# Gates' one-hot products in the float32r form with 256 columns per token, a gather rate of 0.39 per load, x turned beside the first projection

## The chip, the cores and the metric

The kernel runs on one core of a Trainium2 chip. The metric is the device time in microseconds of one execution; several executions are taken and the median is quoted. A profile comes from one further execution. Five engines appear in it: PE (TensorE: matmuls, with its weight loads listed as PEld), DVE (VectorE), ACT (ScalarE), POOL (GpSimd) and SP (SyncE), the last of which only issues transfers here.

## The reference

One block of a transformer over 256 tokens of width 2048, all in 32-bit floats. Four steps follow one another, each adding to the residual `h` but the last:

```
n = rmsnorm(x, g);  proj = n @ w_in                      # 2048 x ~10,500
y_a = dilated windowed attention (3 dilations, 4 heads of 128)
y_b = gates * (compressed, selected and windowed attention; 16 heads of 64, 2 key groups)
h = x + (sigmoid(m0) * (y_a @ w_up_a) + sigmoid(m1) * (y_b @ w_up_b)) @ w_out
h = h + cross attention over 256 memory rows
# experts: 8 heads, 16 of 128 x 128 = 16384 experts per head and token
xn = rmsnorm(h);  eid, g = top16 of the product keys, softmax of the scores
h = h + sum_e g * gelu(xn . u_tab[eid]) * v_tab[eid]     # 128 experts per token
out = rmsnorm(h)
```

The two expert tables `u_tab` and `v_tab` have 16384 rows of 2048 floats each, 134 MB per table.

## The kernel before, in words

A planner orders the instructions: the program is traced in Python, each instruction gets its place by the order of tracing and by when the planner's model takes its inputs to be ready, and the engines then work through their queues strictly in the planned order. `issue_after` (used through `tc_after`) keeps an instruction behind a given one on the same engine.

**Start (`phase1`, L287 on).** x comes in four blocks of 512 columns, each in two token halves (L301). `gain_T` (L255) turns a block with eight transposes on PE; ACT writes the rounded high part times the gain, DVE the remainder, so that x stands as a pair of float32r operands (`nh`, `nl`), features on the partitions. All four blocks are turned first; then come the sums of squares (L215, L217), the reciprocal root (L228, POOL) and the row of it along the free axis (`rstd_row`, L232). The transposes need the constant `ident`, fetched on POOL's queue (L89).

**Projections.** `proj_col` (L184) and `proj_tok` (L155) run over units of 256 features: a 512 KB weight load into one of three `raw` buffers, a split on ACT (`wh`, L149) and DVE (`wl`, L150), and three products per tile (high x high, high x low, low x high). After each unit `tick` lets one background generator take a step: the turning of the memory input (`mem_T`, L350), then attention. In `item_b` (L577) one step computes the scores of four pairs (two key groups of 64 features on partitions 0 to 63 and 64 to 127, two branches), and a later one the values: products with 64 output rows, key group 0 on rows 0 to 63, key group 1 on 64 to 127, in the order group, branch, key tile (L581, L589, L630).

**Experts (`phase2`, L841).** The first 160 tokens (NA) go through both tables in full, as dense products: 256 loads of 512 KB per table, 8 matmuls of 160 columns to a load in 32-bit form (two records each). The products' results are multiplied with gates spread over all 128 x 128 experts (`spread`, L1065): for each token, a one-hot matrix of 128 x 128 for the first key and one for the second, weighted with the gate, are built on DVE (L1077, L1078), multiplied on PE (L1080, two records) into PSUM, four tokens to a bank, and taken out by ACT (L1085, L1087) or, where a table product is there already, by a multiplication on DVE (L1089, L1091). A tick takes one group of four tokens; there are 40 groups, spaced to end at load 236 of the first table.

The other 96 tokens are handled by indirect gathers: 96 gathers of 128 rows x 8 KB (1.05 MB) from each table, issued on POOL (L993), into four buffers. A gather of the first table is followed by a dot product on DVE (L998), one of the second by a weighted sum (L1008). A dot is traced three gathers after its fetch. With the row fetch and a fold near the end the list has 194 steps. `gtick` (L1046) runs after each load and takes `RATE` = 0.415 steps per load in the first table; at load 256 the rate is set so that the remaining steps are spread over 250 loads of the second table. The count `done` begins at 3. A gather waits for the matmul last issued at its place in the trace (`paced`, L973).

Table loads go on SP's queue into eight buffers (three `raw`, five others; `load`, L1166), each issued when PE has freed a buffer. Seven more loads of the first table are fetched during the last projections (L1107). The fold (L1018) adds the first gathered group's sums into the residual by matmuls while the second table is still running; the residual and the final gains are fetched back during the second table (L1235).

Of the kernel before, what the change touches and what calls it, by code (L numbers as in the profile page):

```python
# [9 lines left out]
F32 = mybir.dt.float32  # L10
# [19 lines left out]
NA = 160  # L30
# [5 lines left out]
RATE = 0.415  # L36
# [25 lines left out]
def setup(tc, I, out):  # L62
# [26 lines left out]
    nc.gpsimd.dma_start(c.ident[:], I["cst"][:, 0:128])  # L89
# [192 lines left out]
def phase1(c):  # L282
# [24 lines left out]
    for nb in range(4):  # L307
        last = gain_T(c, lambda hf, nb=nb: xsrc(hf, nb), N, 0, nb, c.pj, "pj")
    with tc_after(c, last):
        for nb in range(4):  # L310
            for hf in range(2):
                sumsq(c, ss, hf, nb, xsrc(hf, nb), tmp)
    rs0 = rstd_of(c, ss, "n0")
    row0 = rstd_row(c, rs0, trp, "tr", "row0")

    wq = I["w_in"]
    tk = lambda: tick(c)
    first_x(c, N)


    aq, ak, av = [], [], []
    for g in range(3):
        aq.append(page([128, 4, 256], f"aq{g}"))
    free.extend(s for _, s in xs)
# [4 lines left out]

    def to_cols(t, row):  # L330
        def f(i, ps):
            nc.vector.tensor_mul(t[:, 2 * i:2 * i + 2, :], ps[:], row[:, None, :].to_broadcast([128, 2, 256]))
        return f
# [16 lines left out]
    def mem_T():  # L350
        for _ in range(6):
            yield
        for nb in range(4):
            nc.sync.dma_start(mem[nb][0][:],
                              I["mem"][:, nb * 512:nb * 512 + 512].rearrange("(h p) f -> p h f", p=128))
            for _ in range(3):
                yield

        nc.sync.dma_start(dmask[:], cst[:, 384:1408].rearrange("p (a b) -> p a b", a=4))
        nc.sync.dma_start(cmask[:, 0:128], cst[:, 256:384])  # L360
        nc.sync.dma_start(cmask[:, 128:678], cst[:, 1408:1958])
        yield
        for nb in range(4):
            for q in range(2):
                gain_T(c, lambda hf, nb=nb: msrc(hf, nb), M, 2, nb, trp, "tr", (q,))
                yield
                yield
            for hf in range(2):
                sumsq(c, ssm, hf, nb, msrc(hf, nb), tmp)
            yield  # L370
        norm_m["rs"] = rstd_of(c, ssm, "nm")
        norm_m["row"] = rstd_row(c, norm_m["rs"], trp, "tr", "rowm")
        yield

    c.bg.append(mem_T())
    for g in range(3):
        proj_col(c, lambda u, b=g: wq[b, u], KT, N, to_cols(aq[g][0], row0), tk)
# [199 lines left out]
    def item_b(hf, r, sh):  # L577
# [3 lines left out]
        pairs = [(j, kt) for j in range(4) for kt in range(hf + 1)]  # L581
        v = {}

        def scores():
            sc = [scp.tile([128, 2, 256], F32, name="sc") for _ in range(2)]
            for g in range(2):
                p = slice(g * 64, g * 64 + 64)
                for br in range(2):
# [252 lines left out]
def phase2(c):  # L841
# [223 lines left out]
    def spread():  # L1065
# [3 lines left out]
        wtb = state["wtb"] = wbp.tile([128, 128 - NE1, NA], F32, name="wtb")  # L1069
        c.rate, c.n_tick = (NA // 4 + 1) / (236 - state["unit"]), 0  # L1070
        for n0 in range(0, NA, 4):
            gp = skp.tile([128, 4, 128], F32, name="gp")
            for j in range(4):
                n = n0 + j
                oh1 = sp.tile([128, 128], F32, name="oh1", bufs=6)
                oh2 = sp.tile([128, 128], F32, name="oh2", bufs=6)
                nc.vector.tensor_scalar(oh1[:], c.iota[:], eT[0][:, n:n + 1], None, ALU.is_equal)  # L1077
                nc.vector.tensor_scalar(oh2[:], c.iota[:], eT[1][:, n:n + 1], eT[2][:, n:n + 1],  # L1078
                                        ALU.is_equal, ALU.mult)
                nc.tensor.matmul(gp[:, j, :], oh1[:], oh2[:], start=True, stop=True)  # L1080
            gv = gp[:].rearrange("p n e -> p e n")
# [328 lines left out]
```

## Time and profile before

| | |
|---|---|
| time, median of 3 runs | 2163.99 us (2160.7 to 2164.49) |
| profiled execution, its own time | 2163.59 us |
| its span, first to last instruction | 2161.8 us, 36357 instructions |
| PE busy | 2119.6 us, 98% |
| PEld busy | 1999.1 us, 92% |
| DVE busy | 1250.0 us, 58% |
| ACT busy | 565.8 us, 26% |
| POOL busy | 261.7 us, 12% |
| moved by DMA | 642.15 MB, mean 297 GB/s |
| mean granted TensorE clock | 0.995 of 2.4 GHz |

The busy share counts the time in which an engine has an instruction in work. Matmuls overlap in PE's pipeline and their ends are modelled, so a PE that shows 100% can still be fed faster or slower; the spacing of its records tells its pace. The stages lie one behind the other: the first projection to about 43 us, the projections and both attentions to 545, the up, output, cross-attention and routing projections to 957, the first expert table to 1571.5, the second to 2131, and the end. The gates' products run from 1158.5 to 1513 us, inside the first table. A time for a group of instructions is busy time; idle time before it is put down to what was waited for.

### The profile page before, as it was taken

The page shows a single profiled execution, that of the slowest core. Times are in us where ns is not written, and L with a number is a line of the kernel's source. Part 1 is how long each engine was busy: PE and PEld are TensorE (multiplying, and loading weights), DVE is VectorE, ACT ScalarE, POOL GpSimd, SP SyncE. Part 2 cuts the span into 40 slices and gives each one's busy share as a digit, 9 for nine tenths or more (in the row PEclk, how much of TensorE's full clock was granted, in tenths as well). Part 3 has the DMA queues.
Part 4 walks back from the last instruction along what each step waited for, and adds up shares of the span by engine and source line. Part 5 has one row for each costly group of instructions (what it writes and reads, how often), then busy time and mean ns, then how long its engine had stood idle before and what let it go on. Part 6 is the DMA issues. An engine that isn't in the chain of part 4 may idle for free.

```text
span 2161.8 us, 36357 instructions
## 1 busy us (share of the span) xinstructions
PE 2119.6 (98%) x14602; PEld 1999.1 (92%) x14602; DVE 1250.0 (58%) x2326; ACT 565.8 (26%) x1277; POOL 261.7 (12%) x253
## 2 busy tenths in 40 slices
PE   8999999999999999999998999999999999999997
PEld 7998998778888888999998999999999999998996
DVE  5555655776575656766896666766443333333334
ACT  5445444556545555422111111000000000000001
POOL 0000000000000000013222121122221111111111
PEclk9999999999999999999999999999999999999999
DMA  7566545434655556588999999999999999998995
GB/s 246 176 195 190 163 137 171 146 127 137 195 175 188 186 168 219 198 267 346 401 408 405 401 397 395 401 403 391 413 414 412 412 414 413 411 410 337 411 403 200
DMA packets 151977, 642.15 MB, mean 297 GB/s; under 512 B 16928, under 2 KB 19136, under 8 KB 126848
## 3 DMA queue, kind: packets, MB, share of 16 engines
q1 hardware_dynamic: 120560, 425.99, 54.6%
q0 software_dynamic: 30528, 212.76, 24.6%
q8 instruction: 114, 1.87, 0.4%
q10 hardware_dynamic: 720, 1.08, 0.1%
q14 instruction: 55, 0.45, 0.1%
HBM read 635.57 MB, written 4.19 MB: 296 GB/s over the span
## 4 chain that ended last, share of the span: by engine, by line
PE 74%; issue 13%; DMA 6%; DVE 3%; POOL 3%; ACT 1%; POOLq 0%; ACTq 0%; DVEq 0%
PE up L1191 20%; PE y_b L1220 7%; PE pj L168 7%; PE pj L169 7%; PE pj L170 7%; PE pj L204 5%; PE pj L205 5%; PE pj L203 5%; PE y_s L1220 4%; DMA ga<-in_ur_dram,idx 3%; POOL ga L993 2%; PE gp L1080 1%; DVE ga L998 1%; DMA raw<-in_v_dram 1%; DMA ga<-in_vr_dram,idx 1%
## 5 line engine op out<-in xcount | busy, mean ns | idle before, releaser
L150 DVE TENSOR_TENSOR wl<-raw,wh 128x512 fp32r<-128x512 f32 (+1 forms) x576 | 391.2, 684 | 287.5 <-ACT wh L149 280.8
L1191 PE MATMUL up<-xr,raw 128*128 128x160 f32 x3968 | 549.3, 299 | 7.9 <-DMA raw<-in_u_dram 6.4
L1191 PEld LDWEIGHTS up<-xr,raw 128*128 128x128 f32 x3968 | 540.7, 190 | 10.0 <-DMA raw<-in_u_dram 6.2
L149 ACT CAST wh<-raw 128x512 fp32r<-128x512 f32 (+1 forms) x576 | 351.9, 616 | 400.7 <-PE pj L204 164.1
L1008 DVE SCALAR_TENSOR_TENSOR acc<-ga,a,acc 128x2048 f32<-128x2048 f32 x94 | 221.1, 2352 | 372.5 <-DMA ga<-in_vr_dram,idx 372.5
L998 DVE SCALAR_TENSOR_TENSOR ga<-ga,gx 128x2048 f32<-128x2048 f32 x96 | 219.9, 2290 | 148.8 <-DMA ga<-in_ur_dram,idx 148.5
L1220 PE MATMUL y_b<-wta,raw 128*128 128x160 f32 x1520 | 220.6, 300 | 1.7 <-DMA raw<-in_v_dram 1.7
L1220 PEld LDWEIGHTS y_b<-wta,raw 128*128 128x128 f32 x1520 | 210.8, 190 | 3.2 <-DMA raw<-in_v_dram 2.9
L205 PE MATMUL pj<-nh,wl 128*128 128x256 f32 x576 | 163.5, 285 | 0.2 <-DVE wl L150 0.2
L204 PE MATMUL pj<-nl,wh 128*128 128x256 f32 x576 | 163.6, 284 | 0.0
L993 POOL DMA_INDIRECT ga<-in_ur_dram,idx x96 | 120.2, 1252 | 352.5 <-PE up L1191 145.3
L993 POOL DMA_INDIRECT ga<-in_vr_dram,idx x96 | 100.3, 1045 | 503.0 <-PE y_b L1220 438.2
L203 PE MATMUL pj<-nh,wh 128*128 128x256 f32 x558 | 160.0, 287 | 0.0
L1220 PE MATMUL y_b<-wtb,raw 128*128 128x160 f32 x1040 | 151.8, 300 | 0.0
L168 PE MATMUL pj<-wh,nh 128*128 128x512 f32 (+1 forms) x384 | 150.0, 392 | 0.0
L1256 ACT COPY ysb<-y_s 128x480 f32<-128x480 f32 x1 | 0.6, 560 | 564.4 <-PE y_s L1220 564.4
L1220 PEld LDWEIGHTS y_b<-wtb,raw 128*128 128x128 f32 x1040 | 144.6, 190 | 3.7 <-issue 3.7
L169 PE MATMUL pj<-wl,nh 128*128 128x512 f32 (+1 forms) x384 | 147.5, 384 | 0.3 <-DVE wl L150 0.2
L170 PE MATMUL pj<-wh,nl 128*128 128x512 f32 (+1 forms) x384 | 147.0, 383 | 0.0
L1220 PE MATMUL y_s<-wta,raw 128*128 128x160 f32 x912 | 136.6, 299 | 1.4 <-DMA raw<-in_v_dram 1.4
L1220 PEld LDWEIGHTS y_s<-wta,raw 128*128 128x128 f32 x912 | 127.9, 190 | 2.1 <-DMA raw<-in_v_dram 2.1
L205 PEld LDWEIGHTS pj<-nh,wl 128*128 128x128 f32 x576 | 110.7, 193 | 1.4 <-DVE wl L150 0.7
(346 smaller groups left out, 2933.4 us busy)
## 6 DMA issues: line engine op xcount, KB each, us to landing
raw<-in_v_dram SPq DMA_DIRECT2D x256, 512.0 KB, 12.1
raw<-in_u_dram SPq DMA_DIRECT2D x249, 512.0 KB, 7.7
raw<-in_w_in_dram SPq DMA_DIRECT2D x160, 512.0 KB, 3.6
raw<-in_w_out_dram SPq DMA_DIRECT2D x32, 512.0 KB, 3.4
raw<-in_w_pq_dram SPq DMA_DIRECT2D x32, 512.0 KB, 4.3
raw<-in_w_up_b_dram SPq DMA_DIRECT2D x16, 512.0 KB, 3.4
raw<-in_w_xkv_dram SPq DMA_DIRECT2D x16, 512.0 KB, 3.4
raw<-in_w_up_a_dram SPq DMA_DIRECT2D x8, 512.0 KB, 3.4
```

The source lines that it names most:

```text
L149: c.last_act = nc.scalar.copy(h[:, :cols], raw[:, k, :cols]).ins
L150: c.last_sub = nc.vector.tensor_sub(l[:, :cols], raw[:, k, :cols], h[:, :cols].bitcast(F32)).ins
L168: nc.tensor.matmul(o, xh[:, s], h[:, :cols], start=kt == 0, stop=False)
L169: nc.tensor.matmul(o, xh[:, s], l[:, :cols], start=False, stop=False)
L170: c.last_mm = nc.tensor.matmul(o, xl[:, s], h[:, :cols], start=False, stop=kt == nk - 1).ins
L203: nc.tensor.matmul(o, h[:, s], xh, start=False, stop=False)
L204: nc.tensor.matmul(o, h[:, s], xl, start=False, stop=False)
L205: c.last_mm = nc.tensor.matmul(o, l[:, s], xh, start=False, stop=kt == nk - 1 and j % 2 == 1).ins
L993: paced(nc.gpsimd.indirect_dma_start(out=t[:], out_offset=None, in_=table, in_offset=bass.IndirectOffsetOnAxis(ap=g["idx"][:, i:i + 1], ax ...
L998: nc.vector.scalar_tensor_tensor(t[:], t[:], 1.0, g["x"][:], ALU.mult, ALU.mult, accum_out=g["a"][:, i:i + 1])
L1191: c.last_mm = c.last_sub = nc.tensor.matmul(ps[j][:, 0:NA], raw[:, k, j * 128:j * 128 + 128], x, start=kt == 0, stop=kt == KT - 1).ins
L1220: c.last_mm = c.last_sub = nc.tensor.matmul(o, raw[:, d // 4 % 2, d % 4 * 128:d % 4 * 128 + 128], wt, start=e == 0 and d % 3 == 0, stop=e ...
```

## The change

Six edits. `RATE` becomes 0.39. `ident` is fetched on SP's queue. The first of x's four blocks is turned before the first projection, the other three inside it (at its units 1, 3 and 5), with the sums of squares at unit 6 and the row at unit 7; the transposes' PSUM banks are four others than the projection's. That first projection takes no background steps, and `mem_T` no longer skips six. In `item_b` the two key groups alternate. In `spread` the gate is split once into a rounded high part and a remainder (`ghl`); for four tokens DVE builds the first one-hots in one operation, the second ones in one, and multiplies the second by both parts in two; PE multiplies in float32r form with 256 columns per token (high and low side by side), two tokens to a bank; ACT copies the low half out and DVE adds the high half, and the rest works from that sum in SBUF. The float32r operands and the sum lie in buffers that the weight splits used.

```diff
-RATE = 0.415
+RATE = 0.39
@@ setup
-    nc.gpsimd.dma_start(c.ident[:], I["cst"][:, 0:128])
+    nc.sync.dma_start(c.ident[:], I["cst"][:, 0:128])
@@ phase1
-    for nb in range(4):
-        last = gain_T(c, lambda hf, nb=nb: xsrc(hf, nb), N, 0, nb, c.pj, "pj")
-    with tc_after(c, last):
-        for nb in range(4):
-            for hf in range(2):
-                sumsq(c, ss, hf, nb, xsrc(hf, nb), tmp)
-    rs0 = rstd_of(c, ss, "n0")
-    row0 = rstd_row(c, rs0, trp, "tr", "row0")
+    stats = {}
+    turns = Banks(c.pp, ["tr", "pv", "s0", "s1"])
+
+    def x_T(nb):
+        stats["last"] = gain_T(c, lambda hf: xsrc(hf, nb), N, 0, nb, turns, "tx")
+
+    def ahead(u):
+        if u in (1, 3, 5):
+            x_T((u + 1) // 2)
+        if u == 6:
+            with tc_after(c, stats["last"]):
+                for nb in range(4):
+                    for hf in range(2):
+                        sumsq(c, ss, hf, nb, xsrc(hf, nb), tmp)
+            stats["rs"] = rstd_of(c, ss, "n0")
+        if u == 7:
+            stats["row"] = rstd_row(c, stats["rs"], trp, "tr", "row0")
...
+    x_T(0)
     first_x(c, N)
...
+    proj_col(c, lambda u: wq[0, u], KT, N, lambda i, ps: to_cols(aq[0][0], stats["row"])(i, ps), lambda: None, ahead)
+    rs0, row0 = stats["rs"], stats["row"]
...
     def mem_T():
-        for _ in range(6):
-            yield
...
-    for g in range(3):
+    for g in (1, 2):
         proj_col(c, lambda u, b=g: wq[b, u], KT, N, to_cols(aq[g][0], row0), tk)
@@ item_b
-        pairs = [(j, kt) for j in range(4) for kt in range(hf + 1)]
+        pairs = [(2 * g + br, kt) for br in range(2) for kt in range(hf + 1) for g in range(2)]
...
-            for g in range(2):
-                p = slice(g * 64, g * 64 + 64)
-                for br in range(2):
+            for br in range(2):
+                for g in range(2):
+                    p = slice(g * 64, g * 64 + 64)
                     nc.tensor.matmul(sc[g][:, br, :nk], bq[r // 4][0][p, r % 4, q0:q0 + 128],
                                      kvT[p, 2 + br, 0:nk], start=True, stop=True)
@@ spread
+        ghl = sp.tile([128, NA, 2], F32, name="ghl")
+        gh = sp.tile([128, NA], R, name="gh")
+        nc.scalar.copy(gh[:], eT[2][:])
+        nc.scalar.copy(ghl[:, :, 0], gh[:].bitcast(F32))
+        nc.vector.tensor_sub(ghl[:, :, 1], eT[2][:], gh[:].bitcast(F32))
...
-            gp = skp.tile([128, 4, 128], F32, name="gp")
-            for j in range(4):
-                n = n0 + j
-                oh1 = sp.tile([128, 128], F32, name="oh1", bufs=6)
-                oh2 = sp.tile([128, 128], F32, name="oh2", bufs=6)
-                nc.vector.tensor_scalar(oh1[:], c.iota[:], eT[0][:, n:n + 1], None, ALU.is_equal)
-                nc.vector.tensor_scalar(oh2[:], c.iota[:], eT[1][:, n:n + 1], eT[2][:, n:n + 1],
-                                        ALU.is_equal, ALU.mult)
-                nc.tensor.matmul(gp[:, j, :], oh1[:], oh2[:], start=True, stop=True)
-            gv = gp[:].rearrange("p n e -> p e n")
+            e1, e2 = [eT[i][:, n0:n0 + 4][:, :, None].to_broadcast([128, 4, 128]) for i in range(2)]
+            row = c.iota[:, None, :].to_broadcast([128, 4, 128])
+            oh1 = c.hlp.tile([128, 4, 128], R, name="oh1", tag="wh")
+            hot = sp.tile([128, 4, 128], F32, name="hot")
+            oh2 = [c.hlp.tile([128, 2, 2, 128], R, name="oh2", tag="wl") for _ in range(2)]
+            nc.vector.tensor_tensor(oh1[:], row, e1, op=ALU.is_equal)
+            nc.vector.tensor_tensor(hot[:], row, e2, op=ALU.is_equal)
+            gs = c.hlp.tile([128, 4, 128], F32, name="gs", tag="wh")
+            low = sp.tile([128, 4, 128], F32, name="low")
+            for i in range(2):
+                nc.vector.tensor_tensor(oh2[i][:], hot[:, 2 * i:2 * i + 2, None, :].to_broadcast([128, 2, 2, 128]),
+                                        ghl[:, n0 + 2 * i:n0 + 2 * i + 2, :, None].to_broadcast([128, 2, 2, 128]),
+                                        op=ALU.mult)
+                gp = skp.tile([128, 2, 2, 128], F32, name="gp")
+                for j in range(2):
+                    nc.tensor.matmul(gp[:, j].rearrange("p a b -> p (a b)"), oh1[:, 2 * i + j, :],
+                                     oh2[i][:, j].rearrange("p a b -> p (a b)"), start=True, stop=True)
+                nc.scalar.copy(low[:, 2 * i:2 * i + 2, :], gp[:, :, 1, :])
+                nc.vector.tensor_add(gs[:, 2 * i:2 * i + 2, :], low[:, 2 * i:2 * i + 2, :], gp[:, :, 0, :])
+            gv = gs[:].rearrange("p n e -> p e n")
```

## Rows read from the trace of the kernel before

**Rows 1.** Busy us (records) of each engine by stretch; clock, DMA share, GB/s.
```profile
60.00:100.00 40.00, 40.00 (x333) 39.82 (x333) 24.00 (x39) 19.18 (x35) 0.00 (x0) 1.00 0.58 173
18.00:20.00 2.00, 1.84 (x9) 1.68 (x9) 2.00 (x6) 2.00 (x7) 0.00 (x0) 1.00 1.05 392
...
1158.50:1513.00 354.50, 354.37 (x2661) 353.93 (x2662) 236.98 (x567) 35.62 (x203) 76.02 (x61) 1.00 1.00 398
1513.00:1571.50 58.50, 57.94 (x427) 57.70 (x426) 27.06 (x27) 4.41 (x18) 12.99 (x11) 1.00 1.02 413
1571.50:1960.00 388.50, 385.41 (x2821) 383.21 (x2819) 143.19 (x66) 0.00 (x0) 66.47 (x66) 1.00 1.02 412
1960.00:1980.00 20.00, 17.95 (x97) 13.40 (x96) 6.47 (x6) 0.00 (x0) 0.94 (x1) 0.91 0.65 242
```

**Rows 2.** Waits of PE, 957 to 1160: us in total, times, longest.
```profile
PE up L1191 <- DMA raw<-in_u_dram: 6.4, 6, 1.4
...
PE gp L1080 <- DVE oh L1078: 0.8, 1, 0.8
```

**Rows 3.** Chain that ended last, 1160 to 1180: start us, us, what.
```profile
1160.12 8.70 PE up L1191 x64
1168.82 0.89 PE gp L1080 x8
```

**Rows 4.** DVE's groups, 1158.5 to 1513: busy us, mean ns, idle before.
```profile
L998 DVE SCALAR_TENSOR_TENSOR ga<-ga,gx 128x2048 f32<-128x2048 f32 x60 | 137.5, 2291 | 113.5 <-DMA ga<-in_ur_dram,idx 113.3
L1078 DVE TENSOR_SCALAR oh<-iota,eT,eT 128x128 f32<-128x128 f32 x159 | 55.1, 347 | 0.0
L1077 DVE TENSOR_SCALAR oh<-iota,eT 128x128 f32<-128x128 f32 x158 | 47.4, 300 | 2.2 <-PE gp L1080 2.2
```

**Rows 5.** Groups by line and shape, whole span: busy us, mean ns, idle before.
```profile
L915 DVE TENSOR_TENSOR eq<-fl,iota 128x512 f32<-128x512 f32 x16 | 10.9, 680 | 0.1
...
L594 DVE SCALAR_TENSOR_TENSOR S<-dmask,sc 128x256 f32<-128x256 f32 x16 | 6.1, 415 | 0.0
```

**Rows 6.** DMA issues from 4.8, 1160, 1600 and 1980 us: count, KB, us to landing.
```profile
raw<-in_w_in_dram SPq DMA_DIRECT2D x1, 512.0 KB, 8.4
...
raw<-in_u_dram SPq DMA_DIRECT2D x141, 512.0 KB, 7.2
ga<-in_ur_dram,idx POOLq DMA_INDIRECT x59, 8.8
...
raw<-in_v_dram SPq DMA_DIRECT2D x81, 512.0 KB, 14.1
wta<-h POOLq DMA_DIRECT2D x4, 512.0 KB, 9.2
...
raw<-in_v_dram SPq DMA_DIRECT2D x55, 512.0 KB, 8.0
```

**Rows 7.** Instructions in order of time, from 0: start us, us, what.
```profile
4.89 2.35 SPq L141 DMA_DIRECT2D raw<-in_w_in_dram  x3
...
15.82 0.64 ACT L149 CAST wh<-raw 128x512 fp32r<-128x512 f32 x1
...
16.52 0.79 PE L200 MATMUL pj<-xz,wh 128*128 128x512 f32 x1
```

**Rows 8.** Chain that ended last, 40 to 795: start us, us, what.
```profile
43.33 0.24 PE pj L200
...
438.34 0.59 PE pv L630 x8
...
473.90 1.06 PE sc L589 x4
...
482.50 1.51 PE pv L630 x16
...
484.60 1.07 PE sc L589 x8
...
784.50 1.80 PE sc L762 x8
```

More of the change, by code (lines that the diff above doesn't have):

```diff
@@ L306, in phase1, with to_cols, f @@
     ss = new_ss(c, "ss0")
-    for nb in range(4):
-        last = gain_T(c, lambda hf, nb=nb: xsrc(hf, nb), N, 0, nb, c.pj, "pj")
-    with tc_after(c, last):
-        for nb in range(4):
-            for hf in range(2):
-                sumsq(c, ss, hf, nb, xsrc(hf, nb), tmp)
-    rs0 = rstd_of(c, ss, "n0")
-    row0 = rstd_row(c, rs0, trp, "tr", "row0")
+    stats = {}
[13 more added lines that the diff above has]
+            stats["row"] = rstd_row(c, stats["rs"], trp, "tr", "row0")
     wq = I["w_in"]
     tk = lambda: tick(c)
+    x_T(0)
     first_x(c, N)
     aq, ak, av = [], [], []
+    def to_cols(t, row):
+        def f(i, ps):
+            nc.vector.tensor_mul(t[:, 2 * i:2 * i + 2, :], ps[:], row[:, None, :].to_broadcast([128, 2, 256]))
+        return f
     for g in range(3):
         aq.append(page([128, 4, 256], f"aq{g}"))
+    proj_col(c, lambda u: wq[0, u], KT, N, lambda i, ps: to_cols(aq[0][0], stats["row"])(i, ps), lambda: None, ahead)
+    rs0, row0 = stats["rs"], stats["row"]
     free.extend(s for _, s in xs)
@@ L328, in phase1 @@
         av.append(page([128, 2, 512], f"av{g}"))
[L330 to L333, printed above, removed]
     def to_tok(t, rs):
```

## The prediction

> **What bounds the kernel now.** I read the page's parts 1 and 2 first (PE 98% busy, DMA digit 9 from the middle on), then busy time by stage, because the change sits in stages with different limits. In [rows 1] PE issues without a gap from 1158.5 to 1513 us (the stretch with the gates' products) and almost so from 1571.5 to 1960 (the second table), while the DMA engines move 398 and 412 GB/s. So two limits lie close together: PE's own pace, and a transfer rate that the stages that want more than they get hold at 412 to 413 GB/s. Where PE waited at all is short: 6.4 us for the first table's loads, all before the spread of the gates [rows 2], and in 1571.5 to 1960 some 4.9 us (388.5 less 2821 x 0.136). The chain of waits gives the pace: 64 table records take 8.70 us (0.136 each, 16 per load, 2.176 per load), then the 8 records of four tokens' gates 0.89 us [rows 3]. The time between the issue of a load and its landing shows the slack: eight buffers hold 17.4 us of PE work (8 x 2.176); a load lands after 7.2 us during the spread, after 14.1 us in 1600 to 1780 and after 8.0 us past 1980 [rows 6]. The second table's early part is thus the place nearest to starving.
>
> **1. Products in the other form.** Removed: per group of four tokens 8 records, 0.89 us. Added: four products of 256 columns with rounded operands. The projections run just such products: 333 in 40.00 us, 0.120 each [rows 1]. Four take 0.48; 0.41 saved, 40 groups: **-16.4 us**, all on the path, since PE has no gap there. Bounds: 0 (another limit takes over) to -16.4.
>
> Does DMA keep up? A group now takes 354.5/40 = 8.86 us, of which 7.97 is loads, 3.66 of them. With 0.39 gathers of 1.049 MB to a load of 0.524 MB, that is 3.66 x 0.933 MB in 8.45 us, 404 GB/s, under 412; with 0.415 it would be 415. So the lower rate is what makes room.
>
> Does DVE? Before, 237 us busy of 354.5, and 113.5 idle before the dot products for their gathered rows [rows 1, 4]. The removed one-hots were 55.1 + 47.4 us, 2.56 per group. The four operations of 512 elements that replace them (two comparisons, two multiplications) I price at 0.68, the nearest comparison with two broadcast operands, and the two sums of 256 elements from PSUM at 0.415 [rows 5]: 3.55 per group, +0.99, over 40 groups +40. About four dot products leave the stage (-9). So 268 of 338 us, 79%: it fits if the waits for gathered rows shrink from 113.5 to 70. They should, being DVE arriving early: a dot is traced three gathers after its fetch. But DVE works in order: behind a dot that waits stand the next group's one-hots, behind these PE's product, behind that the loads' products. Also new: DVE's sum waits for ACT's copy of the low half, which waits for PE; ACT is nearly idle (35.6 us of 354.5 [rows 1]), and the next group is over 8 us away. The two PSUM banks are both used by one group now, with the same 8 us to empty. I take **+2 us** (bounds 0 to +47, the rival below). Rounding the gates once costs two copies and a subtraction before the first group, under 1 us.
>
> The Trainium skill, VectorE: DVE Perf Modes, "Side-by-side: where the cycles go", speaks against this part: a 32-bit operation with one tensor source can run at two elements a cycle from SBUF, one with two tensors cannot. By its 0.96 GHz alone, as an estimate, 1024 elements at two a cycle become 2560 at one, 0.53 against 2.67 us per group; the sum would then add 85 us to DVE, 313 of 338. The trace's mean of 0.300 for 128 elements against 0.680 for 512 [rows 4, 5] says that the fixed part outweighs the mode.
>
> **2. Rate 0.415 to 0.39.** Ahead of the spread about 80 loads run with two gathers less: 2.1 MB, 5.1 us at 413 GB/s, against 6.4 us of waiting [rows 2]: **-5 us** (0 to -6.4). The six gathers saved in all go to the second table: it had (194 - 108)/250 = 0.344 per load, now (194 - 102)/250 = 0.368. That is 0.910 MB per 2.176 us, 418 GB/s against 412 moved [rows 1]: 1.3% of 388.5 us, 5 us more waiting. Against it the stretch 1513 to 1571.5 builds less backlog: it needs 429 instead of 441 GB/s, 2.3 instead of 4.0 us behind. From the fold on (1960 to 1980, 242 GB/s because PE stands) there is slack again. So **+3 us**; bounds 0, and +15 if each of the six gathers (2.54 us) turns into waiting. The 2 MB of the residual that is fetched there [rows 6] loads the same stretch before and after alike.
>
> **3. x turned beside the projection.** Before, the first product starts at 16.52, because ACT's queue holds the turned blocks' casts ahead of the first weight cast at 15.82 [rows 7]. The weights landed at 4.89 + 8.4 = 13.3 [rows 6, 7], so the start can move to about 14.3: 2.2 us. But 24 of the 32 transposes, outside until now, go inside: 24 x 0.111 = 2.7 us (that is a 128-column record, from 0.89/8 [rows 3]). PE steps at 0.22 per product at 18 to 20 us against 0.120 later [rows 1], so each may cost twice that. Gaps while PE waits for the weights may swallow a third of them. The sums of squares come at the seventh unit, the row at the eighth: a wait there would stand before the last unit's products. The constant's load moves to SP's queue ahead of x and the weights: 64 KB, some 0.2 us later for the weights; the transposes that wait for it are no longer what the first product waits for. The memory's loads start two units later in trace order, off the path. Sum **-1 us**, bounds -4 to +3; the second projection's first product, 43.33 before [rows 8], shows it.
>
> **4. Order of the two key groups.** The two groups use different halves of PE's rows (scores) or columns (values). [Rows 8]: eight value records of the first token half take 0.59, about 4 x 0.111 + 0.15, so the halves already overlap there; sixteen of the second take 1.51 where 8 x 0.111 + 0.15 = 1.04 would be full overlap. Alternation should give that: 8 items x 0.47 = 3.8. Eight score records of 256 columns take 1.07, as few as four of a single group (1.06); so those overlap already, and only an item split into two fours, 1.06 + 1.06, can gain 0.9. **-4.5 us**. Bounds: +8 (if every change of half costs that 0.15, seven more in eight items) to -6.
>
> A rule of the Trainium skill bears on it: TensorE: Matmul & The Clock Gate, "The mechanism", has matmuls start and end strictly in program order. By that the score block would take 7 x 0.225 + 0.15 = 1.7 instead of 1.07 and alternation would win another 8 x 0.66 = 5 us, a sum of 2137; the trace disagrees with it (0.225 is 1.80/8 of a full-height record [rows 8]), so I leave those 5 us out.
>
> **Sum.** The profiled execution took 2163.59 (span 2161.8, 1.8 around it), 0.4 under the median 2163.99. -16.4 + 2 - 5 + 3 - 1 - 4.5 = -21.9: 2141.7, and **2142** against the median.
>
> **Rivals.** (a) Given back in the second table: all six gathers become waiting, +15 instead of +3: 2154. For it: that stretch moves 412 and already waits; against: the loads land early again after 1960 (8.0 us), so the end has slack. (b) DVE becomes the bound of the spread, slower than before: the 113.5 us of waiting don't shrink, because gathers are issued at PE's steps and land 8.8 us later [rows 6] whatever DVE does. Then the stage takes 354.5 + 40 - 9 = 385.5 us, +31 instead of -14.4; with the other parts (-10.5, the second table's extra waiting gone): 2163.6 + 31 - 10.5 = 2184. It decides once more than about 95 of the 113.5 us remain. For it: those waits are a third of the stage now; against: PE waited for a one-hot only once, 0.8 us at the stage's start [rows 2]. The rule of the Trainium skill, VectorE: DVE Perf Modes, cited in part 1, points the same way.  (c) The form isn't faster on PE (0.22 per 256-column product, as at the start): no gain from part 1, 2158; nothing but the first 20 us speaks for it. (d) The score blocks gain too, because the overlap seen in 1.07 us was the planner's luck in some items: another 5 us, 2137; the value of 0.59 to 0.65 in every item of the first half speaks against it.
>
> **Chances.** Forecast 0.57 (2132 to 2149), (d) 0.05, (a) 0.18, (b) 0.10, (c) and mixtures 0.10, of which 0.04 end without a change. Faster by over 0.2% (4.3 us, about what a measurement tells from no change) 0.86, within 0.04, slower 0.10. The range leaves out (b) and the upper end of (c): 2131 to 2160.
>
> **What would show it.** Right: gates' products 0.12 apart; loads before 1158.5 with 1 to 2 us of PE waiting; a load of the second table landing after 14 us or more up to the fold; DVE's idle time before dots near 70 us; sixteen value records in about 1.05; the second projection near 42. Wrong: PE waiting for the one-hot operands or the sums in the spread (b), PE waits for the second table's loads over 12 us in all (a), value records still 1.5.

## The result and the profile after

The changed kernel takes 2177.21 us (median of 12 runs, 2168.86 to 2182.04) against 2162.12 beside it: ratio 1.007, 95% interval 1.0061 to 1.0078. It is slower, by 15 us; the forecast was 2142 us, faster. The profiled execution has a span of 2174.8 us, 13.0 more than before's.

Where the 13.0 us arise is read from four times of the trace: the first product of the first table, the first and last of the gates' products, the first product of the second table, and the start of the last 24 products of that table that follow one another, behind which the close begins.

| | before | after | forecast | measured |
|---|---|---|---|---|
| start to first table | 957.2 | 953.1 | -5.5 | -4.1 |
| first table up to the gates' products | 201.4 | 203.8 | -5 | +2.4 |
| stretch of the gates' products | 353.7 | 355.8 | -14.4 | +2.1 |
| rest of the first table | 57.5 | 56.6 | 0 | -0.9 |
| second table | 561.4 | 572.9 | +3 | +11.5 |
| close | 30.6 | 32.6 | 0 | +2.0 |

So the early edits did what was said, and three terms failed: the two that should have won something in the first table, and the price in the second. The busy time by stretch of the kernel after, over the windows of [rows 1] (us, then busy us and records of PE, weight loads, DVE, ACT, POOL, then clock, DMA share, GB/s):

```profile
1158.50:1513.00 354.50, 343.74 (x2493) 341.86 (x2493) 286.06 (x476) 69.01 (x281) 67.81 (x57) 0.98 0.97 383
1513.00:1571.50 58.50, 58.50 (x433) 58.50 (x432) 26.29 (x34) 5.45 (x20) 14.95 (x11) 1.00 1.02 412
1571.50:1960.00 388.50, 380.24 (x2760) 375.23 (x2759) 150.39 (x68) 0.00 (x0) 85.96 (x70) 1.00 1.02 413
1960.00:1980.00 20.00, 19.79 (x146) 19.55 (x145) 7.30 (x4) 0.00 (x0) 3.10 (x3) 1.00 1.03 412
1980.00:2000.00 20.00, 16.24 (x77) 10.88 (x76) 7.14 (x6) 0.00 (x0) 0.77 (x1) 0.83 0.57 215
```

In the first line PE has gaps that it did not have before (344 of 354.5 busy, against 354.4), and even its busy time buys less, since the granted clock's mean is 0.98. Transfers fell from 398 to 383 GB/s: DMA is not what holds this stretch. In the third line DMA is full as before, and 61 records fewer fit in (2760 against 2821).

The chain that ended last shows that the products are as cheap as forecast: four in 0.47, where eight took 0.89 [rows 3]. It also shows the wait ahead of the first (start us, us, what):

```profile
1139.59 12.68 DMA ga<-in_ur_dram,idx
...
1152.30 2.30 DVE ga L1009 x2
1154.60 0.60 DVE oh L1094
...
1156.89 0.80 PE gp L1104 x2
...
1177.77 0.47 PE gp L1104 x4
```

A dot waits for its gathered row; behind it on DVE stand the first one-hots, and PE waits for them. PE's waits, 957 to 1160 us (us in total, times, longest), answer to [rows 2]:

```profile
PE gp L1104 <- DVE oh L1099: 5.4, 1, 5.4
PE up L1218 <- DMA raw<-in_u_dram: 3.2, 3, 1.3
PE sc L1162 <- DVE idx L967: 1.5, 1, 1.5
```

The loads' waiting fell by 3.2 us as it should (6.4 before), and one wait for DVE took it all back (0.8 before). From 1160 to 1570, where PE before had waited 0.6 us in all:

```profile
PE up L1218 <- ACT wta L1231: 7.8, 2, 4.1
PE up L1218 <- ACT wtb L1231: 2.0, 2, 1.4
PE gp L1104 <- ACT wtb L1114: 0.8, 2, 0.6
```

L1231 is the evacuation of the first table's products from PSUM, by ACT, which I had called nearly idle. ACT's copies of the gates now wait for DVE's sum, where they had waited for PE's product; they and DVE's multiplication by the gates also take longer, now that they read the sum in SBUF and not the product in PSUM. Before (1158.5 to 1513 us: busy us, mean ns, idle ahead and what ended it), then after:

```profile
L1087 ACT COPY wtb<-gp 128x208 f32<-128x208 f32 (+9 forms) x39 | 11.9, 305 | 121.5 <-PE gp L1080 121.5
L1089 DVE TENSOR_TENSOR wta<-wta,gp 128x304 f32<-128x304 f32 (+9 forms) x39 | 16.5, 423 | 0.0
```
```profile
L1114 ACT COPY wtb<-gs 128x208 f32<-128x208 f32 (+9 forms) x39 | 19.3, 495 | 65.6 <-DVE gs L1107 65.6
L1116 DVE TENSOR_TENSOR wta<-wta,gs 128x304 f32<-128x304 f32 (+9 forms) x39 | 24.2, 620 | 0.0
L1009 DVE SCALAR_TENSOR_TENSOR ga<-ga,gx 128x2048 f32<-128x2048 f32 x57 | 130.5, 2290 | 55.4 <-DMA ga<-in_ur_dram,idx 54.9
```

The last line answers to [rows 4]. One of PE's waits instruction by instruction, first ACT, then PE (start us, us, engine, line, what, in brackets the idle time ahead and what ended it):

```profile
1205.06 0.28 ACT L1231 ACTIVATE wta<-up 128x136 f32<-128x136 f32 x1
1209.47 0.39 ACT L1112 COPY wta<-gs 128x112 f32<-128x112 f32 x1 [4.13 <-DVE gs L1107]
1209.76 0.55 ACT L1114 COPY wtb<-gs 128x208 f32<-128x208 f32 x1
1210.21 0.18 ACT L1228 ACTIVATE gl<-up 128x24 f32<-128x24 f32 x1
```
```profile
1203.42 3.15 PE L1218 MATMUL up<-xr,raw 128*128 128x160 f32 x22
1210.62 8.73 PE L1218 MATMUL up<-xr,raw 128*128 128x160 f32 x42 [4.05 <-ACT wta L1231]
```

and DVE, whose sum the copy at 1209.47 awaits:

```profile
1205.87 2.29 DVE L1009 SCALAR_TENSOR_TENSOR ga<-ga,gx 128x2048 f32<-128x2048 f32 x1 [1.65 <-DMA ga<-in_ur_dram,idx]
...
1208.09 0.69 DVE L1099 TENSOR_TENSOR oh<-hot,ghl 128x512 fp32r<-128x512 f32 x1
1208.69 0.75 DVE L1107 TENSOR_TENSOR gs<-low,gp 128x256 f32<-128x256 f32 x2
```

The reader is to follow it backwards. PE at 1206.57 needs a PSUM bank. Its evacuation stands in ACT's queue at 1210.21, behind a copy of the gates' sum that ACT can't start until 1209.47. The sum stands on DVE behind a dot of 2.29 us that waited 1.65 for its gathered row, and behind the second multiplication of the one-hots. And when PE resumes it does 42 records in 8.73 us, 0.208 each instead of 0.136: some 3 us more. The granted clock tells why:

```profile
1180.00:1200.00 20.00, 20.00 (x151) 20.00 (x150) 16.66 (x32) 5.03 (x18) 4.74 (x4) 1.00 1.01 409
1200.00:1220.00 20.00, 15.95 (x98) 15.70 (x98) 12.23 (x20) 2.94 (x14) 1.97 (x2) 0.83 0.74 284
1220.00:1240.00 20.00, 16.27 (x109) 16.03 (x108) 14.10 (x24) 3.73 (x16) 4.05 (x3) 0.92 0.86 331
1240.00:1260.00 20.00, 20.00 (x150) 20.00 (x150) 12.49 (x24) 4.22 (x17) 5.01 (x4) 1.00 0.93 346
```

Part of these 40 us ran at the lower of the clock's two levels (1.2 and 2.4 GHz). In 1200 to 1240 PE does 207 records where a full 40 us hold 301: 12.5 us lost, of which the two waits for `wta` above were 7.8.

The second table's price is read from what the two DMA queues moved in 1571.5 to 1960 (packets, MB, share). q1 carries the table's loads, q0 what POOL issues: the gathers, and the six fetches of the residual and the last gain. After, then before:

```profile
q1 hardware_dynamic: 24731, 90.06, 57.9%
q0 software_dynamic: 10059, 70.09, 43.9%
...
wta<-h POOLq DMA_DIRECT2D x4, 512.0 KB
...
wta<-in_norm_final_dram POOLq DMA_DIRECT2D x2, 512.0 KB
```
```profile
q1 hardware_dynamic: 25402, 92.49, 59.6%
q0 software_dynamic: 9665, 67.25, 42.0%
```

Either way about 160 MB move. The six fetches are the same before; 64 gathers are issued there against 60. So 2.8 MB more of gathers leave 2.4 MB less for loads.

### The profile page after: what moved, and what is told of

Read it like the earlier page. It is cut to its first block, busy times and chain, and to the rows that moved or that the text cites. A ratio compares the mean times of both kernels' runs of the same rounds, so it can differ in the third digit from the quotient of the medians.

```text
span 2174.8 us, 36020 instructions
## 1 busy us (share of the span) xinstructions
PE 2109.0 (97%) x14442; PEld 1983.9 (91%) x14442; DVE 1311.2 (60%) x2247; ACT 601.5 (28%) x1359; POOL 282.1 (13%) x252
## 4 chain that ended last, share of the span: by engine, by line
PE 70%; DMA 11%; issue 10%; DVE 5%; POOL 3%; ACT 1%; POOLq 0%; DVEq 0%; ACTq 0%
PE up L1218 16%; PE y_b L1247 8%; PE pj L168 7%; PE pj L169 7%; PE pj L170 7%; PE pj L204 5%; PE pj L205 5%; DMA ga<-in_ur_dram,idx 5%; PE pj L203 5%; PE y_s L1247 4%; DMA raw<-in_v_dram 3%; POOL ga L1004 2%; DMA ga<-in_vr_dram,idx 2%; DVE ga L1009 2%; DMA raw<-in_w_pq_dram 1%
## 5 line engine op out<-in xcount | busy, mean ns | idle before, releaser
L1218 PE MATMUL up<-xr,raw 128*128 128x160 f32 x3968 | 556.1, 301 | 14.0 <-ACT wta L1231 8.7
L1218 PEld LDWEIGHTS up<-xr,raw 128*128 128x128 f32 x3968 | 547.3, 192 | 16.4 <-ACT wta L1231 10.5
L1004 POOL DMA_INDIRECT ga<-in_vr_dram,idx x96 | 120.5, 1256 | 459.0 <-PE y_b L1247 419.1
```

What stands on the lines that cost most here:

```text
L1004: paced(nc.gpsimd.indirect_dma_start(out=t[:], out_offset=None, in_=table, in_offset=bass.IndirectOffsetOnAxis(ap=g["idx"][:, i:i + 1], ax ...
L1218: c.last_mm = c.last_sub = nc.tensor.matmul(ps[j][:, 0:NA], raw[:, k, j * 128:j * 128 + 128], x, start=kt == 0, stop=kt == KT - 1).ins
```

## The experiments

Ratios are to the kernel before on the same chip, with the 95% interval. "First table" is the time from its first product to the second table's first, "second table" from there to the start of its last 24, both from the profiled run (before: 612.6 and 561.4; after: 616.2 and 572.9). A profiled run can lie some us off its kernel's median, so differences of 2 or 3 us between parts of two such runs say little.

**Which part costs what.** First the rate alone, in the kernel before.

```
-RATE = 0.415
+RATE = 0.39
```

> The kernel before with the gather rate 0.39 and nothing else changed. Theory A: waits for the first table's loads fall by 3 to 5 us, the second table gets longer by 9 to 12: 2168 (2164 to 2172), slower than before. Rival C (only the total counts): 2162 as before. If the lower rate helped, as the forecast had it for the first table alone: 2159.

Ratio 1.0058 (1.0045 to 1.0071), 2176.78 us: by the ratio slower by 12.5 (9.7 to 15.3; the medians differ by 15.0), about twice what I then expected. First table 615.1, second 571.3. Its load waits ahead of the gates fell to 3.0, but the first product waits 4.8 for its one-hots, as in the kernel after; and the second table's stretch of [rows 1] has 64 records fewer than before:

```profile
1571.50:1960.00 388.50, 379.88 (x2757) 374.82 (x2756) 149.96 (x68) 1.06 (x4) 83.71 (x69) 1.00 1.02 413
```

Then the kernel after with the rate put back (`RATE = 0.415`):

> The changed kernel with the gather rate back at 0.415, nothing else undone. Theory A (two separate losses: in the spread, ACT's copies of the gates wait for DVE's sum and hold the table products' evacuation behind them, some 18 us; in the second table, the six gathers that the lower rate moves there all become waiting, some 9 to 12 us): the second table (from its first product to the last 24-record run before the end) back from 576 to about 565 us, the first table 0 to 5 us longer, the whole near 2169 (2165 to 2173). Rival B (DVE's throughput is the bound, whatever the rate): 2175 or more, since DVE gets more dot products in the spread. Rival C (the transfers' total sets the end, so the place of a gather does not matter): unchanged, 2175 to 2179.

1.0053 (1.0040 to 1.0066), 2174.37. The second table comes back to 563.5; the first grows to 629.3, which no theory had. PE's waits there, 953 to 1550 (0.6 us more are for `gl`):

```profile
PE up L1218 <- ACT wtb L1231: 13.0, 5, 4.1
PE up L1218 <- ACT wta L1231: 8.7, 5, 3.4
PE up L1218 <- DMA raw<-in_u_dram: 6.1, 5, 1.4
PE gp L1104 <- DVE oh L1099: 2.0, 1, 2.0
```

The first product waits less (2.0 us for 5.4), and the evacuations are waited for twice as long as in the kernel after (21.7 against 10.7 us). The number of dots doesn't explain it (58 from 1160 to 1512, against 56); where they fall between the sums might, which stays open.

Then the kernel after with the products of before in place of the new ones:

```
+            gp = skp.tile([128, 4, 128], F32, name="gp")
+            for j in range(4):
...
+                nc.tensor.matmul(gp[:, j, :], oh1[:], oh2[:], start=True, stop=True)
+            gv = gp[:].rearrange("p n e -> p e n")
...
```

> The changed kernel with the spread of the gates as it was before (32-bit products, one-hots by single operations, gates taken straight from PSUM); rate 0.39, x turned beside the projection and the new order of the key groups stay. Theory A: PE's waits in the spread vanish, the spread lasts 353 us as before, the gain of 4 us ahead of the first table stays, the first table's load waits shrink by 3 to 5, the second table loses 9 to 12: about 2163 (2159 to 2168). Rival B: the same, since the old products load DVE less. Rival C (the end is set by the total of transfers alone): no different from the changed kernel, 2175 to 2179.

1.0032 (1.0021 to 1.0043), 2168.80. First table 615.8, second 570.2, and 6.7 us of waiting for the first one-hots. The new products as they stand, 0.42 us cheaper a group, are thus a loss beside this kernel (1.0032 against 1.007). In the profiled runs the two first tables are equal (615.8 and 616.2): all that the products save there, 40 x 0.42 = 16.8 us, is taken back. Of the 8 us between the ratios these two runs show 4.7, most of it (2.7) in the second table, for which I have no cause.

The early edits without the new products or the new rate (the last kernel with `RATE = 0.415`), then each by itself in the kernel before:

> The kernel before with only its early part changed: x turned beside the first projection, and the keys' order of the window's scores and values; old products, 0.415 gathers a load. Theory A (the early part is worth about -4 by where the first table starts, 953 against 957 us, and the loss lies in the rate and in the products' chain through ScalarE): first table starts at 953, its 201 us, the spread's 354 and the second table's 561 stay, total 2157 to 2159 against 2161.7. Rival (the early start is given back, since the gathers don't come earlier and the gates' chain waits as long as before): first table starts at 953 but the first gates' product stays at 1158, total 2161 to 2163.

0.9964 (0.9952 to 0.9976), 2154.85. The first table starts at 951.2 and is 611.7 long.

```
-    for nb in range(4):
-        last = gain_T(c, lambda hf, nb=nb: xsrc(hf, nb), N, 0, nb, c.pj, "pj")
...
+    x_T(0)
     first_x(c, N)
...
+    proj_col(c, lambda u: wq[0, u], KT, N, ..., lambda: None, ahead)
```

> The kernel before with x turned beside the first projection and nothing else changed. Theory: the second projection's first product starts 1.8 us earlier (43.33 to about 41.6), and nothing between there and the first table gives it back: total -1 to -2.5, 2159.5 to 2161. Rival (the early start also ends lower-clock time or waits that the start of the first table shows): -4 or more.

0.9994 (0.9985 to 1.0003), 2160.87: between 3.2 us less and 0.6 more, so no change is shown. The second projection starts at 42.31 (43.33 before), the first table at 957.6 (957.2 before): the microsecond gained at the start doesn't show there in this run.

```
-        pairs = [(j, kt) for j in range(4) for kt in range(hf + 1)]
+        pairs = [(2 * g + br, kt) for br in range(2) for kt in range(hf + 1) for g in range(2)]
...
-            for g in range(2):
-                p = slice(g * 64, g * 64 + 64)
-                for br in range(2):
+            for br in range(2):
+                for g in range(2):
+                    p = slice(g * 64, g * 64 + 64)
```

> The kernel before with only the new key order in the window's scores and values. Theory: the second half's blocks give 0.44 to 0.46 us each for eight heads' scores and values as forecast, the first table starts about 4 earlier: total -3.5 to -5, about 2157.5. Rival (the pairs were beside each other already, the order does nothing): 2161 to 2163.

0.9986 (0.9977 to 0.9996), 2157.42. Values and scores in order of time on PE, items of the second half, in this kernel and then in the kernel before:

```profile
472.60 0.70 PE L589 MATMUL sc<-kvT,bq 64*128 64x256 f32 x4
...
490.32 1.09 PE L630 MATMUL pv<-PT,vtok 128*64 128x128 f32 x16
...
491.93 1.14 PE L589 MATMUL sc<-kvT,bq 64*128 64x256 f32 x8
```
```profile
473.83 1.13 PE L589 MATMUL sc<-kvT,bq 64*128 64x256 f32 x4
...
502.15 1.58 PE L630 MATMUL pv<-PT,vtok 128*64 128x128 f32 x16
...
504.25 1.14 PE L589 MATMUL sc<-kvT,bq 64*128 64x256 f32 x8
```

Sixteen values give 0.49, eight items 3.9. Eight scores in one run give nothing. But where an item's scores are split into two runs of four, each run takes 0.70 in place of 1.13, 0.86 an item; the kernel before has one such item. The two early edits together give a ratio 0.0036 under 1, one by one 0.0006 and 0.0014; the intervals overlap.

**Why cheaper products cost time.** Theory: ACT's copies of a group's sum stand in front of evacuations, so a late sum stops PE. Then it helps to use a group's result one step later (below, the late use):

```
+        def apply(n0, gs):
+            gv = gs[:].rearrange("p n e -> p e n")
...
         for n0 in range(0, NA, 4):
+            if due:
+                apply(*due)
...
+            due = (n0, gs)
```

> The changed kernel in which each group's gates are used one step later: the sums of group n are copied by ACT and multiplied by DVE at the step that builds group n+1, so that ACT's copies find their sum long done. Same operations, same count. Theory A: PE's waits for ACT in the spread (10.6 us by the trace) and the slow stretches behind them go; the spread shrinks from 356 to about 340 us, the second table stays near 576: 2161 (2156 to 2166). Rival B (DVE's throughput): no gain, 2175 to 2179, PE waiting for the one-hots instead. Rival C (transfers): PE's waits move to the table loads, 2170 or more.

1.0002 (0.9988 to 1.0016), 2164.57, at 0.39. PE's waits for the evacuations of the first table are gone from the gates' stretch, which falls from 355.8 to 337.4 us. Not all of that is won: the last step now only uses a result, so the last product comes a step earlier, and the rest of the table grows from 56.6 to 63.8. The first table as a whole falls from 616.2 to 609.4, in a profiled run that is the slowest of the twelve (2170.40). And the first product now waits 11.3 us (PE's waits, 953 to 1550):

```profile
PE gp L1122 <- DVE oh L1117: 11.3, 1, 11.3
PE gp L1122 <- DVE oh L1112: 3.0, 3, 1.6
PE up L1227 <- DMA raw<-in_u_dram: 1.6, 3, 0.7
```

The same with the rate at 0.415:

> The kernel after with the products' result used one step later (as in the run with that edit at 0.39) and the rate back at 0.415. Theory A (the spread is held by the chain product, VectorE's sum, ScalarE's copies, the evacuations behind them; the rate costs the second table 10): the spread stays near 337 us, the second table comes back from 574 to 563, total about 2154, under both kernels (ratio to before about 0.996). Rival (the 18 us that the late use gained at 0.39 need the thinner gathers, since at 0.415 VectorE's dots again stand before the sums): spread 350 or more, total 2162 or more.

0.9952 (0.9937 to 0.9967), 2151.92: the stretch stays at 338.0, the first table takes 603.6 (629.3 with the results used at once), the second is back at 562.5, and the first one-hots cost 3.7. Then, on top of the late use, one-hots a step ahead of their products, at 0.39 and at 0.415:

```
+        for n0 in range(0, NA + 4, 4):
+            if due:
+                apply(*due)
+            due, was = None, made
+            made = (n0, *hots(n0)) if n0 < NA else None
+            if was:
+                due = products(*was)
+            yield
```

> The kernel after, rate 0.39, with one-hots built one step ahead of the products and the result used one step after them. Theory A (the first product waits 11.3 us in the late version only because its one-hots stand behind a dot that waits for its gather): that wait falls below 2, the stretch from the first table's start to the first product from 208 to about 198, the spread stays 337, the second table 573, total about 2156. Rival (the stretch is set by the dots themselves, and the wait moves on to the sum or to the copies): the stretch shorter but the spread longer by as much, total about 2164.

0.9965 (0.9953 to 0.9977), 2154.21. First table 595.7, the shortest of all, with no wait for one-hots; second 573.1. (With the products a step later in the trace, its parts can't be set beside the others', only their sum.)

> The kernel after with one-hots a step ahead, the result used a step later, and 0.415 gathers a load: all three causes taken away. Theory A: first stretch 198 to 200, spread 337 to 340, second table 563, total 2144 to 2148 (ratio about 0.993). Rival (rate and products compete for VectorE in the spread, so that what one gives the other takes): total 2155 or more, no better than the same kernel at 0.39.

**0.9927 (0.9914 to 0.9940), 2146.50 us**, runs within 1.5 us of each other: faster than both kernels, and called the mended kernel below. First table 597.7, second 565.2. The gates' stretch again has PE almost without gaps and at full clock, transfers at 413 GB/s; PE's waits from 953 to 1550 stand behind it:

```profile
1160.00:1484.00 324.00, 322.12 (x2381) 320.76 (x2379) 282.70 (x469) 67.19 (x274) 92.38 (x57) 1.00 1.02 413
```
```profile
PE up L1236 <- DMA raw<-in_u_dram: 5.6, 7, 1.4
PE gp L1122 <- DVE gs L1125: 1.7, 3, 0.8
PE up L1236 <- ACT gl L1246: 1.1, 1, 1.1
PE up L1236 <- ACT wta L1249: 0.9, 1, 0.9
```

DVE is busy for 283 of these 324 us, 87% (286 of 354.5, 81%, in the kernel after), and PE waits for its sums only 1.7 us.

**Is it DVE's waiting or its work?** Two runs of the kernel after leave out part of the dot products. In the first they are taken of the tokens' rows with themselves, times zero, so that none waits for a gather:

```
-        nc.vector.scalar_tensor_tensor(t[:], t[:], 1.0, g["x"][:], ALU.mult, ALU.mult, ...)
+        nc.vector.scalar_tensor_tensor(g["x"][:], g["x"][:], 0.0, g["x"][:], ALU.mult, ALU.mult, ...)
```

> The kernel after, with the dot products taken of the tokens' rows with themselves (times zero) in place of the gathered rows: same length of work on VectorE, same gathers, but no dot waits for a gather (the output is not the reference's). Theory A (a dot waiting in order for its gathered row holds up the sums of the gates, ScalarE's copies and the evacuations behind them): no waits on evacuations in the gates' stretch, the first gates' product doesn't wait, the first table from 616 to 594 to 600 us, total about 2156. Rival (VectorE's own work, 79% of the stretch, is what delays the sums): the first table stays above 610 us, total 2170 or more.

1.0025 (1.0016 to 1.0035), 2168.17; first table 607.6. Missed, and not a clean test: without the gathers as inputs the dots moved up in DVE's order (the last starts at 1322.0, against 1548.0), into the stretch ahead of the gates, where PE now waits 7.6 us for the first one-hots and 4.0 for the routing. In the gates' stretch itself 2.9 us of waiting for evacuations are left, of 9.8.

In the second the dots cover 1024 of 2048 columns (`t[:, 0:1024]`), and still wait:

> The kernel after, with the dot products over the first 1024 of 2048 columns (the output is not the reference's): each takes 1.15 instead of 2.29 us on VectorE, but still waits for its gathered row. Theory A (the wait, not the work): VectorE's idle time before dots grows by about what its work shrinks, the waits on evacuations are still 4 us or more, the first table 607 to 616 us, total 2166 to 2175. Rival (VectorE's own work): as with dots that don't wait, 594 to 600 us, total about 2156.

1.0016 (1.0007 to 1.0026), 2165.29; first table 605.5. DVE's idle time before dots grows from 110 to 195 us, as its work shrinks by 102, and the evacuations are still waited for 6.2 us. Theory A's figures are missed by 0.7 and 1.5 us on the low side, its rival's by 9 and 5.5; and the profiled run, from which the table's length and the waits come, is the fastest of its ten (2160.69). So neither theory holds alone, though this run lies nearer to A. By the chain shown above a sum is late by the gathered row's delay plus the length of the dot, and each run shortens one of them. How much belongs to each stays open.

**Is more rate better?** The fastest kernel with `RATE = 0.43`:

> The kernel with one-hots ahead and the late use, with 0.43 gathers a load in place of 0.415: about four gathers more beside the first table. Theory (each gather costs what the transfers of its table can't carry: the first table's stretch already moves 413 GB/s, the second table's loads still wait 4.5 us and its fold 3): the first table gets load waits of 4 to 8 us, the second table gives 3 to 5: total 2146 to 2151, no better. Rival (the first table has room still): the second table gives 4 or more and the first nothing: 2142 to 2143.

0.9975 (0.9964 to 0.9987), 2156.20: 10 us worse than at 0.415. The second table gives 4.8 (560.4), the first takes 13.4 (611.1), more than expected and from other places than loads: 3.4 for one-hots, 3.2 for an evacuation, 2.6 and 0.9 for the routing, a clock of 0.99. The load waits themselves fell, from 5.6 to 2.7. So 0.415 is the best of the three rates tried in this order, and not for the reason that the theory gave: what 0.43 loses, it loses by these waits to DVE's queue and to what stands behind it.

## Why the prediction was wrong

**Part 1, "+2" for the stall: failed, the largest error.** The saving per group is right (0.47 for 0.89). Between the mended kernel and the kernel with the early edits and the old products (0.9927 and 0.9964, both at 0.415), the first table differs by 611.7 - 597.7 = 14.0 us; forecast was 14.4. The whole times differ by less, 8.4 us: the second table takes 2.6 back, and the old products' profiled run was the slowest of its six. One-hots ahead with the old products were not run, so the 14.0 isn't the form's alone. But in the order that the change has, at the same rate, it is 629.3: 31.6 us more than mended, and 20.5 at 0.39 (616.2 and 595.7), where I had put +2. The step that failed is the sentence that "ACT is nearly idle", and that "the next group is over 8 us away". I priced ACT by its busy share (35.6 of 354.5 us) and never asked what stands in its queue behind the copies of the sum. Before, those copies waited for PE only; the new form put a DVE sum between them, and so the gathers' lateness, through DVE and ACT, into the path of PSUM banks. I had the first half of the chain (one-hots behind a waiting dot) and looked for its effect on the one-hots; it came through the sum. The late use and the one-hots ahead took that chain away, and the time with it; how much of it is the wait for the gathered row and how much the dot's own length stays open.

**Rival (b) named the wrong resource.** It ended near the result, at 2184, by chance: it got there by DVE's throughput. DVE was busier than I had priced, 286 us for 268. The operations that I had priced cost what I said (0.684 to 0.690 us for 0.68, 0.414 for 0.415); left out was the multiplication by the gates, which reads the sum from SBUF and takes 24.2 us for 16.5, and the rest I can't place. But DVE's waits for gathered rows did shrink, from 113.5 [rows 4] to 55.4, well below the 95 from which (b) decides, and the mended kernel runs its stretch in 324 us with DVE 87% busy.

**Part 2, "-5": failed.** The load waits went as forecast (6.4 to 3.2, and 3.0 with the rate alone). What became late next is a wait I had listed at 0.8 and not followed: the first one-hots: 4.8, 5.4 and 6.7 us in the three kernels at 0.39 with full dots and results used at once, 0.5 to 2.6 in the five such at 0.415; 11.3 against 3.7 in the two with late use. With one-hots ahead that wait is gone, and the first table of the profiled run is 2.0 us shorter at 0.39 (595.7 for 597.7), no more than such runs scatter. Nor do the load waits there follow the rate: 6.5 us at 0.39, 5.6 at 0.415, 2.7 at 0.43.

**Part 2, "+3": failed; the price lies between it and rival (a), +15.** For the six gathers the second table pays 9.9 alone, 7.6 on the early edits, 9.4 in the changed kernel, 11.6 with the late use, 7.9 in the mended kernel. I set the new demand (418 GB/s) against 412 moved and called the difference the price (1.5%, 5.8 us, where I wrote 1.3% and 5). As an estimate from the same rows: before, the demand was 0.524 + 0.344 x 1.049 = 0.885 MB per 2.176 us, 407 GB/s: a surplus of 5 GB/s over 388.5 us, 1.9 MB, which paid for part of the residual and the last gain, 6 x 0.524 = 3.1 MB. The change takes that surplus as well. After: 5.2 GB/s short is 2.0 MB, with the 3.1 MB 5.1 in all, 12.4 us at 413 GB/s; the stretch lost 388.5 - 2760 x 0.136 = 13.1. For the kernel before the same working gives 1.2 MB, 2.8 us, where 4.9 were lost, so it has the size and not the exact figure. "Before and after alike" was true of the residual's bytes and wrong of its price. The forecast slack past 1960 was not there either: the fold only came later, to 1980 to 2000, and the close took 2.0 more in the profiled run, with 1.9 of waiting for DVE (0.2 before).

**Parts 3 and 4: right.** x turned: -1 forecast, the second projection 1.0 earlier; in the whole time, ratio 0.9994 (0.9985 to 1.0003), an effect of that size can't be told from none. Key order: -4.5 forecast, start of the first table at 952.7 instead of 957.2 and 0.9986 (0.9977 to 0.9996); values 3.9 of 3.8, and 0.86 for the item whose scores were split, which the prediction put at 0.9. The other items' scores gain nothing, so rival (d), 5 us more, falls. By the rule of the Trainium skill that I set aside there (TensorE: Matmul & The Clock Gate, "The mechanism", matmuls in strict order) the eight scores would have to take 1.7 us in the old order; the trace has 1.14, in both orders. That speaks against the rule only if PE got the two groups in the order in which they were traced, which no run here shows.

**Rival (c)** falls with 0.47 per group.

## What to carry to other kernels

An engine with a low busy share is free only if nothing urgent stands in its queue behind the instruction you add a wait to: list the queue of every engine on the way from the new producer to the critical one. Such a chain is cured by order at no cost in work (operands built a step early, results used a step late gave 27 us at 0.415, 1.0053 against 0.9927). And when a stage sits at the transfer rate, ask what the surplus that an added byte takes was paying for: six gathers cost the second table 7.6 to 11.6 us, where I had forecast 3 and their full time would be 15.

## What was not expected of the hardware

A stall of 3 to 4 us on TensorE costs more than itself. In the kernel after, a wait of 4.05 us is followed by 42 records at 0.208 us instead of 0.136, with a granted clock of 0.83 for the 20 us around it; with the rate back, a wait of 3.38 by 12 records in 3.38 us, 0.28 each, and 0.91. The first table with the rate back is 31.6 us longer than the mended one at that rate, and the waits listed for it differ by 30.4 - 9.3 = 21.1 us. Of the 10 left the stretches of lower clock are the only sign that I see in the records. They are about as large: in windows of 20 us from 953 on, six of the trace with the rate back have a mean clock of 0.91, and 6 x 20 x 0.09 is 10.8 us, as an estimate; the mended kernel's windows all show 1.00 up to 1590. That the clock accounts for all of it was not tried. The changed kernel's times also scatter more, over 13 us in twelve runs, where the kernel before spans 7 in twelve and the mended one 1.5 in five.

Reading the gates from SBUF costs more than reading them from PSUM. DVE's multiplication of 304 elements takes 0.687 us from the sum in SBUF and 0.463 from the product in PSUM, twenty of each; ACT's copies of the same shapes take 0.495 and 0.305 on average. The prediction had no term for either.
